# A hybrid Mamba-2 and attention trunk on one core: the decays of the scan leave the high-priority block, and the masked scores get a second buffer

## The chip, the core and the metric

The kernel runs on one core of a Trainium2 chip. The metric is the device time of one execution in microseconds (us); smaller is better. The time before is 2582.29 us, the median of three runs (2581.88 to 2584.90).

## What is computed

A trunk of two layers over 2048 tokens of width 1024, all in float32. The first layer is a Mamba-2 mixer (state-space duality), the second is sliding-window attention. The part that the change touches is the scan of the first layer, chunk by chunk (128 tokens) for each of 8 groups of 4 heads:

```python
a_cs = jnp.cumsum(a, axis=-1)
seg = a_cs[..., :, None] - a_cs[..., None, :]
decay = jnp.exp(jnp.where(causal, seg, -jnp.inf))
cb = jnp.einsum('bclgn,bcsgn->bcgls', Cc, Bc)
y_diag = jnp.einsum('bcgrls,bcsgrp->bclgrp', cb[:, :, :, None] * decay, x)
decay_to_end = jnp.exp(a_cs[..., -1:] - a_cs)
states = jnp.einsum('bclgn,bcgrl,bclgrp->bcgrpn', Bc, decay_to_end, x)
```

The states are carried from chunk to chunk, and `y_off` adds what the carried state gives. Ahead of the scan stand the input projection (1024 to 6176 columns), a causal convolution over 4 tokens and a SiLU; behind it a gate, a norm and the output projection.

## The kernel before, in words

**Stages.** By the trace the first layer's projection and scan take about 0 to 1400 us, its output projection up to about 1725, the attention layer the rest. Every large product is done as three products of split numbers: `mm3` issues high by high (L90), high by low (L92) and low by high (L91) on TensorE (PE). Each weight tile is loaded by SP (L148), rounded to its high part by ScalarE (ACT) as `whi` (L150), and the low part `wlo` is made by GpSimd (POOL, L152).

**Loops.** The first stage runs over two halves of the tokens (hf 0 and 1, 1024 tokens each), and in each over 8 groups. For a group, `ssm_proj` projects the tiles x0, x1, B, C and z0, z1; a tile of x, B or C then goes through the convolution: ACT copies it out of PSUM (L742) and starts the sum (L746), VectorE (DVE) adds the taps (L749), ACT and DVE do the SiLU (L752, L753). The scan of group g runs beside the projection of group g+1: `interleave` steps the generator `ssm_scan` as the projection goes on. The scan of the last group (hf 1, group 7) runs beside the first matmuls of the output projection (`u`, L251), whose weights are split by L222 and L223 and whose rows are squared and summed by a reduction on DVE (L239).

**The scan of one chunk.** `stage1` transposes x0, x1 and B on PE and multiplies B by C into one PSUM tile `pt` (L779 to L784). From it come `xd` (DVE, L789), the split of B into `bh` (ACT, L793) and `bl` (DVE, L795), the weighted inputs `xw` (DVE, L798) and their split `xh` (ACT, L801) and `xl` (DVE, L803), and the masked scores `cbm` (DVE, L806). Then come the decays: four Relu on ACT (L809), the exponential of `ab` (ACT, L814) and its product with C on POOL (L815), the exponential of `dec` (ACT, L816) and its product with `cbm` on DVE (L817). `ab` is a row of cumulated decays that SP's DMA spreads over all partitions (L767). `states` multiplies `xh`, `xl`, `bh`, `bl` on PE into `sps`, two chunks at a time; DVE adds the carried state, `hn` (L842, L844), POOL decays it, `hd` (L833). `outputs` multiplies `dec` by `xd` (L856) and `ab` by the state (L861) into `yt`; DVE and POOL finish it (L868, L870).

**What orders the work.** A scheduler orders each engine's instructions when the program is built. It goes by a priority, which is the place in the program; inside `high_priority(offset=60)` an instruction counts as standing 60 places further ahead. In the kernel before that block reaches from L785 to L817. Each engine then runs its own queue strictly in this order.

**Buffers.** `px` is a ring of four 4 KB buffers for the rows of x (`xt`, L107). `rows` (L574) is loaded once, in the first 20 us, with the convolution's weights and biases and the gate's norm (DMAs L575 to L577); PE transposes it (L579, L582), and DVE scales it to `cw`, `cb` and `gn` (L580, L583, L584). In the kernel before, `rows` has 1 KB per partition of its own, and `cbm` has one buffer of 512 bytes.

Of the kernel before, what the change touches and what calls it, by code (L numbers as in the profile page):

```python
# [11 lines left out]
F32 = mybir.dt.float32  # L12
# [3 lines left out]
AF = mybir.ActivationFunctionType  # L16
ALU = mybir.AluOpType
# [4 lines left out]
P = 128  # L22
T = 2048
D = 1024
# [36 lines left out]
class Trunk:  # L61
# [492 lines left out]
    def ssm_consts(self, pool):  # L554
        nc, io = self.nc, self.io

        def bcast(ap, n, name):
            t = pool.tile([P, n], F32, name=name)
            nc.sync.dma_start(t, ap.partition_broadcast(P))
            return t  # L560

        self.abc = bcast(io["ssm_a_log"][0], NH, "abc")
        nc.scalar.activation(self.abc, self.abc, AF.Exp)
        nc.vector.tensor_scalar(self.abc, self.abc, -1.0, None, ALU.mult)
        self.dtb = bcast(io["ssm_dt_bias"][0], NH, "dtb")
        d = bcast(io["ssm_d"][0], NH, "dall")
        self.dch = pool.tile([P, NH // 2], F32, name="dch")
        d2 = d.rearrange("p (t two) -> p t two", two=2)
        nc.vector.tensor_copy(self.dch[0:64], d2[0:64, :, 0])
        nc.vector.tensor_copy(self.dch[64:P], d2[64:P, :, 1])  # L570

        self.cw = pool.tile([P, 4, 32], F32, name="cw")
        self.cb = pool.tile([P, 32], F32, name="cb")
        rows = pool.tile([P, 2, P], F32, name="rows")  # L574
        nc.sync.dma_start(rows[:, 0, :], io["ssm_conv_w"][0].rearrange("k (t p) -> (k t) p", p=P))  # L575
        nc.sync.dma_start(rows[0:32, 1, :], io["ssm_conv_b"][0].rearrange("(t p) -> t p", p=P))
        nc.sync.dma_start(rows[32:48, 1, :], io["ssm_gate_norm"][0].rearrange("(t p) -> t p", p=P))  # L577
        pt = self.tp.tile([P, P], F32, tag="tr", name="pt")
        nc.tensor.transpose(pt, rows[:, 0, :], self.ident)  # L579
        nc.vector.tensor_scalar(self.cw.rearrange("p k t -> p (k t)"), pt, 0.5, None, ALU.mult)  # L580
        pt = self.tp.tile([P, 48], F32, tag="tr", name="pt")
        nc.tensor.transpose(pt, rows[0:48, 1, :], self.ident[0:48, 0:48])  # L582
        nc.vector.tensor_scalar(self.cb, pt[:, 0:32], 0.5, None, ALU.mult)  # L583
        nc.vector.tensor_scalar(self.gn, pt[:, 32:48], 0.5, None, ALU.mult)  # L584
        self.halo = pool.tile([P, 32, 3], F32, name="halo")
        self.hsave = [pool.tile([P, 256], F32, name=f"hsave{g}") for g in range(NG)]
# [169 lines left out]
    def ssm_scan(self, sp, yp, tabs, hf, g, res, yT):  # L756


        nc = self.nc
        dt, acs, cd, w2, atd = (tabs[k] for k in ("dt", "acs", "cd", "w2", "atd"))  # L760
# [9 lines left out]
        def stage1(c):  # L770
            if c > 7:
                return
            ab = abs_[c]
            s, o = divmod(c, 4)
            sl = slice(o * P, (o + 1) * P)
            x0, x1, Bt, Ct = (res[n, s] for n in ("x0", "x1", "B", "C"))
            pt = (yp.tile([P, 4, P], F32, tag="y", name="pt", bufs=2) if c % 2
                  else self.tp.tile([P, 4, P], F32, tag="tr", name="pt"))
            nc.tensor.transpose(pt[:, 0, :], x0[:, sl], self.ident)  # L779
            nc.tensor.transpose(pt[:, 1, :], x1[:, sl], self.ident)  # L780
            last = hf == 1 and c == 7
            if not last:
                nc.tensor.transpose(pt[:, 2, :], Bt[:, sl], self.ident)
            nc.tensor.matmul(pt[:, 3, :], Bt[:, sl], Ct[:, sl], start=True, stop=True)  # L784
            with self.tc.high_priority(offset=60):  # L785
                xv = pt[:, 0:2, :].rearrange("p a (h d) -> p (a h) d", d=64)
                xd = sp.tile([P, 4, 64], F32, tag="xd", name="xd", bufs=4)
                hb = dt[:, c, 4 * g:4 * g + 4].unsqueeze(2).to_broadcast([P, 4, 64])
                nc.vector.tensor_tensor(xd, xv, hb, ALU.mult)  # L789
                bx = None  # L790
                if not last:
                    bh = sp.tile([P, P], F32R, tag="bh", name="bh")
                    nc.scalar.activation(bh, pt[:, 2, :], AF.Copy)  # L793
                    bl = sp.tile([P, P], F32R, tag="bl", name="bl")
                    nc.vector.tensor_tensor(bl, pt[:, 2, :], bh.bitcast(F32), ALU.subtract)  # L795
                    xw = sp.tile([P, 4, 64], F32, tag="xw", name="xw", bufs=1)
                    hb = w2[:, c, 4 * g:4 * g + 4].unsqueeze(2).to_broadcast([P, 4, 64])
                    nc.vector.tensor_tensor(xw, xv, hb, ALU.mult)  # L798
                    xf = xw.rearrange("p h d -> p (h d)")
                    xh = sp.tile([P, 256], F32R, tag="xh", name="xh")  # L800
                    nc.scalar.activation(xh, xf, AF.Copy)  # L801
                    xl = sp.tile([P, 256], F32R, tag="xl", name="xl")
                    nc.vector.tensor_tensor(xl, xf, xh.bitcast(F32), ALU.subtract)  # L803
                    bx = bh, bl, xh, xl
                cbm = sp.tile([P, P], F32, tag="cbm", name="cbm", bufs=1)
                nc.vector.tensor_tensor(cbm, pt[:, 3, :], self.triu, ALU.mult)  # L806
                dec = sp.tile([P, 4, P], F32, tag="dec", name="dec", bufs=4)
                for r in range(4):
                    nc.scalar.activation(dec[:, r, :], ab[:, r, :], AF.Relu, scale=-1.0,  # L809
                                         bias=acs[:, c, 4 * g + r:4 * g + r + 1])  # L810
                ce = None
                if not (hf == 0 and c == 0):
                    ce = ab
                    nc.scalar.activation(ce, ab, AF.Exp)  # L814
                    nc.gpsimd.tensor_tensor(ce, ce, Ct[:, sl].unsqueeze(1).to_broadcast([P, 4, P]), ALU.mult)  # L815
                nc.scalar.activation(dec, dec, AF.Exp, scale=-1.0)  # L816
                nc.vector.tensor_tensor(dec, dec, cbm.unsqueeze(1).to_broadcast([P, 4, P]), ALU.mult)  # L817
            sts.append((xd, bx, dec, ce))

        def states(c):  # L820
# [54 lines left out]
        for c in range(4):  # L875
            load(c)
        stage1(0)
        yield
        stage1(1)
        yield  # L880
        hprev = self.hsave[g] if hf else None
        hd = decayed(0, hprev)
        yield
        for c in range(0, 8, 2):
            sps = states(c)
            h0 = hprev
            h1, hd = state(c, sps[:, 0, :], hd)
            yield
            hprev, hd = state(c + 1, sps[:, 1, :], hd)
            stage1(c + 2)  # L890
            yield
            stage1(c + 3)
            yield
            outputs(c, (h0, h1))
            load(c + 4)
            load(c + 5)
            yield
# [161 lines left out]
```

## Time and profile before

| | |
|---|---|
| median of 3 runs | 2582.29 us (2581.88 to 2584.90) |
| the profiled execution | 2584.72 us, of which the span of the trace is 2583.0 us |
| PE | 2527.8 us busy, 98% |
| DVE | 1673.7 us busy, 65% |
| ACT | 1274.9 us busy, 49% |
| POOL | 921.6 us busy, 36% |
| DMA | 87 GB/s in the mean |
| TensorE's granted clock | 0.995 of full speed in the mean |

The chain that ended last runs over PE for 74% of the span, over DVE for 10%, POOL 5%, ACT and DMA 4% each. The span is the time between the first and the last instruction in the trace; the rest of the execution's own time lies around it. In the views below an instruction has its start, its duration, its engine, its line, its operation, and what it writes and reads; in square brackets stands how long the engine had been idle before it and whose result ended that.

### The profile page before, as it was taken

The page shows a single profiled execution, that of the slowest core. Times are in us where ns is not written, and L with a number is a line of the kernel's source. Part 1 is how long each engine was busy: PE and PEld are TensorE (multiplying, and loading weights), DVE is VectorE, ACT ScalarE, POOL GpSimd, SP SyncE. Part 2 cuts the span into 40 slices and gives each one's busy share as a digit, 9 for nine tenths or more (in the row PEclk, how much of TensorE's full clock was granted, in tenths as well). Part 3 has the DMA queues.
Part 4 walks back from the last instruction along what each step waited for, and adds up shares of the span by engine and source line. Part 5 has one row for each costly group of instructions (what it writes and reads, how often), then busy time and mean ns, then how long its engine had stood idle before and what let it go on. Part 6 is the DMA issues. An engine that isn't in the chain of part 4 may idle for free.

```text
span 2583.0 us, 38760 instructions
## 1 busy us (share of the span) xinstructions
PE 2527.8 (98%) x14083; PEld 2107.9 (82%) x14083; DVE 1673.7 (65%) x3363; ACT 1274.9 (49%) x3195; POOL 921.6 (36%) x817
## 2 busy tenths in 40 slices
PE   7999999999999999999999999999999999999998
PEld 6878888888777888888887888888888888888787
DVE  6677666766776667666678544447777777767422
ACT  5455555555645555555566422324554455545321
POOL 2344444444434454444445222222222112220222
PEclk9999999999999999999999999999999999999999
DMA  4332223223423222222325332234111121111343
GB/s 127 96 86 64 81 76 87 74 70 78 116 62 105 78 83 77 78 78 78 82 78 174 113 101 90 90 128 140 54 54 58 54 78 54 54 32 58 123 146 120
DMA packets 266656, 224.46 MB, mean 87 GB/s; under 512 B 31136, under 2 KB 229984, under 8 KB 266464
## 3 DMA queue, kind: packets, MB, share of 16 engines
q1 hardware_dynamic: 266464, 221.98, 29.2%
q8 instruction: 111, 1.82, 0.3%
q14 instruction: 81, 0.66, 0.1%
HBM read 179.72 MB, written 42.21 MB: 86 GB/s over the span
## 4 chain that ended last, share of the span: by engine, by line
PE 74%; DVE 10%; POOL 5%; DMA 4%; ACT 4%; issue 4%; SPq 0%; POOLq 0%; ACTq 0%; DVEq 0%
PE u L251 19%; PE ps L90 14%; PE ps L92 14%; PE ps L91 14%; DVE sx L749 2%; DMA ab<-atd 2%; POOL wlo L152 2%; PE sc L420 2%; PE yt L856 2%; PE yt L861 1%; PE ot L474 1%; PE ot L478 1%; DVE dec L817 1%; PE tt L453 1%; POOL ab L815 1%
## 5 line engine op out<-in xcount | busy, mean ns | idle before, releaser
L90 PE MATMUL ps<-hi,whi 128*128 128x512 f32 (+1 forms) x1808 | 725.5, 401 | 9.4 <-ACT whi L150 4.7
L92 PE MATMUL ps<-hi,wlo 128*128 128x512 f32 (+1 forms) x1808 | 706.1, 391 | 4.2 <-POOL wlo L152 4.2
L91 PE MATMUL ps<-lo,whi 128*128 128x512 f32 (+1 forms) x1808 | 704.6, 390 | 0.2 <-DVE lo L140 0.2
L92 PEld LDWEIGHTS ps<-hi,wlo 128*128 128x128 f32 x1808 | 340.7, 188 | 80.2 <-POOL wlo L152 6.1
L90 PEld LDWEIGHTS ps<-hi,whi 128*128 128x128 f32 x1808 | 341.2, 189 | 77.9 <-issue 15.9
L152 POOL TENSOR_TENSOR wlo<-wraw,whi 128x1024 fp32r<-128x1024 f32 x114 | 282.6, 2479 | 319.1 <-ACT whi L150 310.6
L749 DVE SCALAR_TENSOR_TENSOR sx<-raw,cw,sx 128x512 f32<-128x512 f32 x384 | 342.9, 894 | 71.3 <-ACT sx L746 66.5
L91 PEld LDWEIGHTS ps<-lo,whi 128*128 128x128 f32 x1808 | 341.6, 189 | 55.2 <-DVE lo L140 0.8
L251 PE MATMUL u<-ol,yh 128*128 128x512 f32 x768 | 239.6, 393 | 1.0 <-DVE ol L223 0.9
L251 PE MATMUL u<-oh,yh 128*128 128x512 f32 x768 | 240.5, 394 | 0.0
L251 PE MATMUL u<-oh,yl 128*128 128x512 f32 x768 | 237.6, 391 | 0.0
L809 ACT ACTIVATE dec<-ab,acs 128x128 f32<-128x128 f32 x512 | 165.4, 392 | 128.9 <-DMA ab<-atd 114.3
L815 POOL TENSOR_TENSOR ab<-ab,sx 128x512 f32<-128x512 f32 x120 | 168.9, 1409 | 154.5 <-ACT ab L814 140.5
L752 ACT ACTIVATE raw<-sx 128x512 f32<-128x512 f32 x128 | 80.6, 630 | 221.4 <-DVE sx L749 221.3
L90 PE MATMUL ps<-qh,hi 128*128 128x384 f32 x512 | 181.1, 355 | 0.0
L870 POOL TENSOR_TENSOR ysb<-ysb,zz 128x256 f32<-128x256 f32 x128 | 108.1, 861 | 197.9 <-DVE ysb L868 197.7
L235 POOL TENSOR_TENSOR yl<-yr,yh 128x1024 fp32r<-128x1024 f32 (+1 forms) x64 | 119.3, 1864 | 161.3 <-ACT yh L233 161.2
L233 ACT ACTIVATE yh<-yr 128x1024 fp32r<-128x1024 f32 (+1 forms) x64 | 54.1, 845 | 242.3 <-PE u L251 189.3
L91 PE MATMUL ps<-ql,hi 128*128 128x384 f32 x512 | 172.1, 337 | 0.9 <-POOL ql L332 0.9
L251 PEld LDWEIGHTS u<-ol,yh 128*128 128x128 f32 x768 | 143.9, 188 | 34.3 <-DVE ol L223 2.6
L92 PE MATMUL ps<-qh,lo 128*128 128x384 f32 x512 | 171.9, 336 | 0.0
L251 PEld LDWEIGHTS u<-oh,yl 128*128 128x128 f32 x768 | 144.5, 188 | 31.4
(213 smaller groups left out, 4527.7 us busy)
## 6 DMA issues: line engine op xcount, KB each, us to landing
wraw<-in_ssm_w_in SPq DMA_DIRECT2D x98, 512.0 KB, 4.1
ab<-atd SPq DMA_DIRECT2D x128, 256.0 KB, 4.6
xt<-in_x SPq DMA_DIRECT2D x32, 512.0 KB, 4.8
yT<-ysb SPq DMA_DIRECT2D x64, 256.0 KB, 2.5
yr<-yT SPq DMA_DIRECT2D x32, 512.0 KB, 4.0
xt<-x SPq DMA_DIRECT2D x32, 512.0 KB, 4.0
oraw<-in_ssm_w_out SPq DMA_DIRECT2D x16, 512.0 KB, 5.9
x<-xt SPq DMA_DIRECT2D x32, 256.0 KB, 2.1
```

The costliest lines, as they stand in the source:

```text
L90: nc.tensor.matmul(ps, sh, mh, start=first, stop=False)
L91: nc.tensor.matmul(ps, sh, ml, start=False, stop=False)
L92: nc.tensor.matmul(ps, sl, mh, start=False, stop=last)
L152: nc.gpsimd.tensor_tensor(lo, raw, hi.bitcast(F32), ALU.subtract)
L233: nc.scalar.activation(yh, yr, AF.Copy)
L235: nc.gpsimd.tensor_tensor(yl, yr, yh.bitcast(F32), ALU.subtract)
L251: nc.tensor.matmul(st["u"][h], y[:, k, :], w[:, j, 512 * h:512 * h + 512], start=k0 + k == 0 and m == 0, stop=k0 + k == kt - 1 and m == 2)
L749: nc.vector.scalar_tensor_tensor(sx, raw[:, j:j + BLK], self.cw[:, j, ct:ct + 1], sx, ALU.mult, ALU.add)
L752: nc.scalar.activation(th, sx, AF.Tanh)
L809: nc.scalar.activation(dec[:, r, :], ab[:, r, :], AF.Relu, scale=-1.0, bias=acs[:, c, 4 * g + r:4 * g + r + 1])
L815: nc.gpsimd.tensor_tensor(ce, ce, Ct[:, sl].unsqueeze(1).to_broadcast([P, 4, P]), ALU.mult)
L870: nc.gpsimd.tensor_tensor(yv, yv, res[f"z{pr}", s][:, sl], ALU.mult)
```

## The change

Three edits. The high-priority block ends behind `cbm`, so that the decays (the four Relu, both exponentials, POOL's product and DVE's product) are ordered by their own place in the program. `cbm` gets two buffers instead of one. `rows` gives up its own memory and takes a buffer of the ring `px`, which it shares with the rows of x. Nothing is computed differently.

```diff
-        rows = pool.tile([P, 2, P], F32, name="rows")
+        rows = self.px.tile([P, D], F32, tag="px", name="rows")[:, 0:2 * P].rearrange("p (a b) -> p a b", a=2)
...
-                cbm = sp.tile([P, P], F32, tag="cbm", name="cbm", bufs=1)
+                cbm = sp.tile([P, P], F32, tag="cbm", name="cbm", bufs=2)
                 nc.vector.tensor_tensor(cbm, pt[:, 3, :], self.triu, ALU.mult)
-                dec = sp.tile([P, 4, P], F32, tag="dec", name="dec", bufs=4)
-                for r in range(4):
-                    nc.scalar.activation(dec[:, r, :], ab[:, r, :], AF.Relu, scale=-1.0,
-                                         bias=acs[:, c, 4 * g + r:4 * g + r + 1])
-                ce = None
-                if not (hf == 0 and c == 0):
-                    ce = ab
-                    nc.scalar.activation(ce, ab, AF.Exp)
-                    nc.gpsimd.tensor_tensor(ce, ce, Ct[:, sl].unsqueeze(1).to_broadcast([P, 4, P]), ALU.mult)
-                nc.scalar.activation(dec, dec, AF.Exp, scale=-1.0)
-                nc.vector.tensor_tensor(dec, dec, cbm.unsqueeze(1).to_broadcast([P, 4, P]), ALU.mult)
+            dec = sp.tile([P, 4, P], F32, tag="dec", name="dec", bufs=4)
+            for r in range(4):
+                nc.scalar.activation(dec[:, r, :], ab[:, r, :], AF.Relu, scale=-1.0,
+                                     bias=acs[:, c, 4 * g + r:4 * g + r + 1])
+            ce = None
+            if not (hf == 0 and c == 0):
+                ce = ab
+                nc.scalar.activation(ce, ab, AF.Exp)
+                nc.gpsimd.tensor_tensor(ce, ce, Ct[:, sl].unsqueeze(1).to_broadcast([P, 4, P]), ALU.mult)
+            nc.scalar.activation(dec, dec, AF.Exp, scale=-1.0)
+            nc.vector.tensor_tensor(dec, dec, cbm.unsqueeze(1).to_broadcast([P, 4, P]), ALU.mult)
             sts.append((xd, bx, dec, ce))
```

On PE the order stays as it was, but for the first 40 us and for some 40 us around 1390. On the other engines most instructions of the scan move by a place or a few. Three places:

**ACT, where the scan of the first group of the second half starts (about 812 to 819 us).** `whi_8032` is the weight tile that PE needs next, `dec_8005` and `ab_7770` belong to the fourth chunk. First the kernel before, then the changed one:

```order
L814 ACTIVATE ab_7770<-ab_7770 128x512
L801 ACTIVATE xh_7941<-xw_7939 128x256
L816 ACTIVATE dec_8005<-dec_8005 128x512
L752 ACTIVATE raw_7872<-sx_7875 128x512
L744 ACTIVATE halo_345<-ps_7888 128x3
L746 ACTIVATE sx_7960<-ps_7888,cb_333,cw_332 128x512
L150 ACTIVATE whi_8032<-wraw_8030 128x1024
```

```order
L746 ACTIVATE sx_7960<-ps_7888,cb_333,cw_332 128x512
L809 ACTIVATE dec_8005<-ab_7770,acs_7718 128x128 x2
L801 ACTIVATE xh_7941<-xw_7939 128x256
L809 ACTIVATE dec_8005<-ab_7770,acs_7718 128x128
L741 ACTIVATE raw_8020<-halo_345 128x3
L150 ACTIVATE whi_8032<-wraw_8030 128x1024
L814 ACTIVATE ab_7770<-ab_7770 128x512
L816 ACTIVATE dec_8005<-dec_8005 128x512
```

Both exponentials of the fourth chunk stand behind the weight tile now. Further ahead, the SiLU's `raw_7806` (L752) stands ahead of the first chunk's two exponentials instead of behind them, and on DVE the SiLU's L753 stands ahead of the first chunk's L817.

**SP, in the first 30 us.** The three DMAs of `rows` and what stands around them:

```order
 L559 DMA dtb<-in_ssm_dt_bias 128x32
 L559 DMA dall<-in_ssm_d 128x32
+L148 DMA wraw<-in_ssm_w_in 128x8x128 x2
+L107 DMA xt<-in_x 128x1024 x2
 L575 DMA rows<-in_ssm_conv_w 128x128
 L576 DMA rows<-in_ssm_conv_b 32x128
 L577 DMA rows<-in_ssm_gate_norm 16x128
-L148 DMA wraw<-in_ssm_w_in 128x8x128
-L107 DMA xt<-in_x 128x1024
-L148 DMA wraw<-in_ssm_w_in 128x8x128
-L107 DMA xt<-in_x 128x1024
```

They stand behind two weight tiles and two rows of x, and they need a free buffer of `px`: the one whose `xt` PE transposes last before them. On PE, L579 stands four products later, and L582 behind the next transposes of x.

**DVE, beside the output projection (about 1369 to 1373 us).** `red_13343` is the reduction of the output projection, `xl_13420` the split of the sixth chunk of the last group:

```order
 L806 TENSOR_TENSOR cbm_13422<-pt_13405,triu_90 128x128
 L734 SCALAR_TENSOR_TENSOR zz_13433<-zz_13433,ps_13302 128x512
+L239 TENSOR_REDUCE red_13343<-yr_13336 128x128
+L803 TENSOR_TENSOR xl_13420<-xw_13416,xh_13418 128x256
 L817 TENSOR_TENSOR dec_13424<-dec_13424,cbm_13422 128x512
-L803 TENSOR_TENSOR xl_13420<-xw_13416,xh_13418 128x256
-L239 TENSOR_REDUCE red_13343<-yr_13336 128x128
 L844 TENSOR_TENSOR hn_13478<-hd_13453,sps_13471 128x256
```

The reduction has moved ahead of the split, and the product of the decays behind it.

## Rows read from the trace of the kernel before

**Rows 1.** The page's first part: busy us, share of the span, instructions of each engine.
```profile
PE 2527.8 (98%) x14083; PEld 2107.9 (82%) x14083; DVE 1673.7 (65%) x3363; ACT 1274.9 (49%) x3195; POOL 921.6 (36%) x817
```

**Rows 2.** Windows of the second half: length, busy by engine, granted clock, DMA share, GB/s.
```profile
840.00:1340.00 500.00, 499.69 (x2952) 413.00 (x2952) 336.95 (x596) 284.35 (x673) 232.67 (x181) 1.00 0.29 79
```

**Rows 3.** What PE waited for, 100 to 1410 us: sum, times, longest.
```profile
PE sps L91 <- DVE xl L803: 4.8, 9, 1.4
PE ps L90 <- ACT whi L150: 4.7, 2, 2.7
PE ps L92 <- POOL wlo L152: 3.9, 2, 2.2
PE sps L90 <- ACT xh L801: 2.4, 4, 0.8
```

**Rows 4.** Timeline of PE and ACT, first scan of the first half.
```profile
118.95 0.39 PE L91 MATMUL sps<-xl,bh 128*128 128x256 f32 x1 [0.73 <-DVE xl L803]
130.86 0.50 PE L90 MATMUL ps<-hi,whi 128*128 128x512 f32 x1 [2.07 <-ACT whi L150]
...
125.89 0.64 ACT L814 ACTIVATE ab<-ab 128x512 f32<-128x512 f32 x1
126.41 0.64 ACT L816 ACTIVATE dec<-dec 128x512 f32<-128x512 f32 x1
127.89 0.63 ACT L752 ACTIVATE raw<-sx 128x512 f32<-128x512 f32 x1 [0.84 <-DVE sx L749]
129.77 1.04 ACT L150 ACTIVATE whi<-wraw 128x1024 fp32r<-128x1024 f32 x1
```

**Rows 5.** Timeline of DVE, ACT, POOL and PE, first scan of the second half.
```profile
807.71 1.38 DVE L817 TENSOR_TENSOR dec<-dec,cbm 128x512 f32<-128x512 f32 x1 [5.58 <-ACT dec L816]
...
817.86 1.05 ACT L150 ACTIVATE whi<-wraw 128x1024 fp32r<-128x1024 f32 x1
...
818.97 0.50 PE L90 MATMUL ps<-hi,whi 128*128 128x512 f32 x1 [2.66 <-ACT whi L150]
821.45 0.66 PE L92 MATMUL ps<-hi,wlo 128*128 128x512 f32 x1 [1.75 <-POOL wlo L152]
```

**Rows 6.** The window after that wait: columns as in rows 2.
```profile
820.00:825.00 5.00, 3.55 (x20) 2.71 (x22) 5.00 (x8) 2.69 (x6) 2.78 (x2) 0.66 0.40 105
```

**Rows 7.** Timeline of DVE and PE, last pair of chunks, group 7 of the first half.
```profile
768.56 0.68 DVE L817 TENSOR_TENSOR dec<-dec,cbm 128x512 f32<-128x512 f32 x1
...
771.60 0.38 PE L90 MATMUL sps<-xh,bh 128*128 128x256 f32 x1 [0.77 <-ACT xh L801]
772.34 0.39 PE L91 MATMUL sps<-xl,bh 128*128 128x256 f32 x1 [0.36 <-DVE xl L803]
```

**Rows 8.** Timeline of ACT and PE, last pair of chunks, group 0 of the first half.
```profile
175.18 0.28 ACT L793 ACTIVATE bh<-pt 128x128 fp32r<-128x128 f32 x1 [2.08 <-DVE xd L789]
...
176.84 0.38 PE L90 MATMUL sps<-xh,bh 128*128 128x256 f32 x1 [0.82 <-ACT xh L801]
177.58 0.39 PE L91 MATMUL sps<-xl,bh 128*128 128x256 f32 x1 [0.36 <-DVE xl L803]
```

**Rows 9.** Timeline of PE, around the first use of `rows`.
```profile
27.95 0.60 PE L136 MATMUL pt<-ident,xt 128*128 128x128 f32 x4
...
30.73 0.33 PE L579 MATMUL pt<-ident,rows 128*128 128x128 f32 x1 [0.27 <-DVE lo L140]
```

**Rows 10.** DMA issues, 0 to 60 us: count, size, us from issue to landing.
```profile
dtraw<-in_ssm_w_in SPq DMA_DIRECT2D x1, 128.0 KB, 2.8
rows<-in_ssm_conv_w SPq DMA_DIRECT2D x1, 64.0 KB, 4.6
```

**Rows 11.** Timeline of DVE and PE, last scan, beside the output projection.
```profile
1370.77 1.96 DVE L239 TENSOR_REDUCE red<-yr 128x128 f32<-128x1024 f32 x1
...
1370.90 0.39 PE L91 MATMUL sps<-xl,bh 128*128 128x256 f32 x1 [0.76 <-DVE xl L803]
1401.77 0.44 PE L90 MATMUL sps<-xh,bh 128*128 128x256 f32 x1 [2.02 <-DVE hn L844]
```

## The prediction

> **What bounds the kernel now.** I read the page's busy times first, then the stages by windows, then what PE waited for, and last the timelines around the few places where it waited. PE is busy for 2527.8 us, 98% of the span [rows 1]; no other engine passes 65%. So a change that leaves PE's work alone can win no more than PE's idle time, and whatever it does on DVE, ACT and POOL counts only where PE waits for it. By stages the case is clearer still: from 840 to 1340 us, which is most of the second half of the scan, PE is busy for 499.69 of 500 us at the full granted clock [rows 2]. In that stretch the other engines are late for nothing. The waits of the whole stretch that the change touches, 100 to 1410 us, are named in one list [rows 3]: PE waits 4.8 us for `xl`, 4.7 for the high part of a weight tile, 3.9 for its low part, 2.4 for `xh`, and once 2.0 us for the state `hn` [rows 11]. That is 17.8 us in all, 0.7% of the run. The list names neither `dec` nor `cbm` nor the scaled `ab`: PE never waits for the decays. What they can cost is only the place that they take in a queue, ahead of something that PE does wait for. The waits lie at four kinds of places: the start of the scan in either half [rows 4, 5], the last pair of chunks of a group [rows 7, 8], the use of `rows` in the first 40 us [rows 9], and the last scan, beside the output projection [rows 11].
>
> A measurement of this kernel can tell about 0.2%, that is 5.2 us, from no change.
>
> **The change part by part.** Nothing is added to or removed from any engine's work, and no DMA is new. The second `cbm` buffer costs nothing by itself: it lets L806 of a chunk run before L817 of the chunk ahead, which it must, since L817 now stands further back. So everything is order, and I go through the places.
>
> *Start of the scan, first half.* PE stood for 2.07 us until the weight tile `whi` was there, which ACT started at 129.77 [rows 4], and later up to 2.2 us for `wlo` [rows 3], which POOL makes from it. In the new order one L814 and one L816 of the fourth chunk stand behind that tile. They start 0.52 us apart [rows 4], so two of them free 1.04 us. ACT's wait of 0.84 us ahead of L752 [rows 4] shrinks too, since the taps on DVE move ahead of other work; that is between 0 and 0.84. The tile comes 1.04 to 1.88 earlier; I take 1.5. POOL now has one L815 less ahead of `wlo`, so it follows the tile. The `xl` of the second chunk moves ahead of a row of x on DVE, which takes away PE's 0.73 us there [rows 4], but PE then arrives sooner at the same missing tile, so I don't count it. Term: -1.5 us; ends 0 and -4.95 (0.73 + 2.07 + 2.15, all three waits gone).
>
> *Start of the scan, second half.* Here DVE stood 5.58 us before L817 until the first chunk's exponential came, which ACT could not begin before `ab` had landed [rows 5]. Behind that L817 in DVE's queue were `cbm` of the next chunk, the SiLU's L753 and the states. Now L752 and L753 go first. ACT's tile `whi` started at 817.86, and PE waited 2.66 us for it and 1.75 more for `wlo` [rows 5]. Again two exponentials (1.04 us) move behind the tile, and ACT uses a part of the time in which it had stood for `ab` for the L752 that stood behind it (0.5 us, as far apart as the exponentials). That is 1.5 us for `whi`, and `wlo` follows. Term: -1.5; ends 0 and -4.41.
>
> *Last pair of chunks, group 7 of the first half.* PE waited 0.77 for `xh` and 0.36 for `xl` [rows 7]. One L817 of 0.68 us that stood in front of the pair's work [rows 7] now stands behind it. I take the 0.7; ends 0 and -1.13. In the other groups the work on DVE ahead of the last `xl` is the same in sum, only the conv's L753 and the seventh chunk's `xd` change places. There the waits are 0.82 + 0.36 in the first group [rows 8] and smaller ones after it. Term for them: 0; ends -2.3 (what is left of the `xl` and `xh` waits) and, above, the slower rival.
>
> *The first 40 us.* The DMAs of `rows` now wait for a buffer of `px`, which is free when the transposes at 27.95 to 28.55 are done [rows 9]. PE reaches L579 four products later than before. Four transposes take 0.60 us, and before PE waited 0.27 there for something else [rows 9], so that is at 30.73 - 0.27 + 0.60, about 31.0. The bounds of the landing: 4.6 us, as the same DMA took before among large transfers, and 2.8 us, as `dtraw` took when little else ran [rows 10]. So `rows` is there between 31.4 and 33.2, and PE stands 0.4 to 2.2 us. The last row of x is still in flight when it starts, but little comes behind it; I take a value nearer to the lower end: +1.0 us; ends 0 and +2.2. The page "DMA: Bandwidth & Descriptors" of the Trainium skill (section on the anatomy of one DMA, a fit for GpSimd's path) has a fixed 2.0 us and bytes over 436 GB/s; as an estimate from that page, 64 KB would take 2.15 us, land at 30.75, and cost PE nothing, so that the sum below would be 1.0 lower. The trace speaks against it here: no DMA of this size in the first 60 us landed that fast, 2.8 and 4.6 [rows 10], so the rows decide. `rows` holds its slot until L582, and the next load into `px` comes long after, so nothing waits for the slot.
>
> *Beside the output projection.* PE waited 0.76 us for the `xl` that ended at 1370.8 [rows 11]. Now the reduction L239, 1.96 us, stands ahead of this `xl`, and an L817 (0.68, as in [rows 7]) behind it: 1.96 - 0.68 = 1.3 us later, all on PE, which already waits. Term: +1.3; ends 0 and +1.96. The wait of 2.02 at 1401.77 for `hn` [rows 11] hangs on POOL, which gets another order of the same work: 0; ends -2.0 and +1.0 (half of what it is, for want of a nearer row).
>
> *The clock.* From 820 to 825, just behind the wait at the second half's start, the granted clock was 0.66 of full, so about 3.4 of these 5 us were at 1.2 GHz and the rest at 2.4 [rows 6]. Half of the 3.4 us, 1.7, is lost. If a wait becomes short the fall may stay away, at either start; if PE stands longer in the first 40 us one may be added. I count 0; ends -3.4 (both starts) and +1.7.
>
> Sum: -1.5 - 1.5 - 0.7 + 1.0 + 1.3 = -1.4 us. The profiled execution took 2584.72, so 2583.3 on its scale; it stood 2.43 above the median of the runs shown. On the median's scale the forecast is **2580.9 us**, no difference that can be measured.
>
> **The rivals.**
>
> *Faster: the starts come clean.* If the weight tiles come early enough that the clock does not fall at either start (-3.4) and the waits of the last pairs go as well (-2.3), 2580.9 becomes 2575.2, and with a little more of the 4.95 and 4.41 at the starts it is below that. For it: at both starts the waiting chain is ACT's queue alone, and it is ACT's queue that gets shorter. Against: 1.5 us out of 4.2 and 4.4 leaves a wait of over 2.5 us at both, and at the second start the clock fell after a wait of that size [rows 5, 6]. Chance 0.16.
>
> *Slower: the last pairs come late.* In 14 of the 16 groups the seventh chunk's `xd` now stands behind the conv's L753, which itself waits for ACT. `bh` on ACT waited for `xd` in the trace [rows 8], and the last `xl` has no slack there (PE waits for it) [rows 8]. If the whole pair slips by that L753, some 0.68 us (the duration of the L817 in [rows 7], which has as many elements), PE loses 14 times 0.68 = 9.5 us: 2590.4. It decides as soon as `xw` is later than now, for the wait is already there. Against: `bl` and `xw` stood behind the L753 in the old order too, and the second half, 499.69 busy of 500, has room [rows 2]. Chance 0.11.
>
> *Nothing happens.* PE's queue is the same between 40 and 1380 us; if the tiles are bound by DMA or by DVE rather than by ACT's exponentials, the starts stay as they are, and the first 40 us and the reduction cancel against the last pair: 2582.3 to 2584. Chance 0.13; it counts as no change, like the forecast itself with 0.60.
>
> **How the numbers follow.** Faster by over 0.2% is the first rival, 0.16; slower by over 0.2% is the second, 0.11; within it lie the forecast and the empty change, 0.60 + 0.13 = 0.73. The range reaches down to the first rival's 2575 and up to the sum with the clock falling in the first 40 us, a full wait for `rows` and the reduction at its upper end (2580.9 + 1.7 + 1.2 + 0.7 = 2584.5), with another 1.5 for the spread of the runs: 2575 to 2586. It leaves out the slower rival and the far end of the faster one.
>
> **What would show it.** PE's waits for `whi` and `wlo` should fall from 8.6 us to between 5 and 6. The wait for `xl` near 1371 should grow from 0.8 to about 2.1, with L239 right ahead of it. L579 should wait for the DMA of `rows` for about 1 us. From 840 to 1340 PE should stay over 499 us busy. The forecast is wrong if new waits for `dec`, `xd` or `xl` appear in that stretch, if the waits at the starts stay, or if the granted clock falls at a new place.

## The result, and the profile after

The change makes the kernel slower: 2615.55 us, the median of four runs (2614.57 to 2617.50), against 2582.63 us for four runs of the kernel before. The ratio is 1.0127, with a 95% interval of 1.0109 to 1.0144: 33 us. The forecast was 2580.9 us, no difference that can be measured.

The page of the changed kernel, its first part (as in [rows 1]):

```profile
span 2613.4 us, 38766 instructions
PE 2541.3 (97%) x14083; PEld 2115.5 (81%) x14083; DVE 1701.2 (65%) x3363; ACT 1275.3 (49%) x3195; POOL 930.2 (36%) x817
```

The span is 30.4 us longer. PE does the same 14083 matmuls, and its busy time has grown by 13.5 us, which is matmuls at the lower clock or drawn out behind a wait; the rest is new idle time. The mean granted clock fell from 0.995 to 0.992; as an estimate from these two figures, some 26 and 42 us ran at 1.2 GHz and the rest at 2.4, so about 8 of the 13.5 us are the clock's. What PE waited for, 100 to 1410 us (the columns as in [rows 3]):

```profile
PE sps L91 <- DVE xl L803: 10.6, 19, 2.0
PE ps L92 <- POOL wlo L152: 7.8, 4, 2.2
PE sps L90 <- ACT xh L801: 7.6, 9, 1.5
PE ps L90 <- ACT whi L150: 5.9, 3, 3.0
```

The waits for `xl` and `xh` have gone from 7.2 to 18.2 us, from 13 to 28 occurrences; those for the weight tiles, which should have shrunk, from 8.6 to 13.7. And the stretch that was full [rows 2] is so no longer (windows; the third row is a window in the first half, the clock stands behind the five busy times):

```profile
840.00:1340.00 500.00, 492.33 (x2860) 404.25 (x2859) 340.36 (x575) 275.11 (x648) 221.93 (x176) 1.00 0.28 77
150.00:420.00 270.00, 265.67 (x1534) 218.54 (x1533) 186.78 (x339) 150.18 (x353) 119.20 (x90) 0.99 0.28 76
340.00:350.00 10.00, 8.17 (x30) 6.26 (x30) 8.45 (x16) 5.49 (x16) 3.55 (x4) 0.83 0.35 105
```

**Where the time went.** PE transposes B once per chunk (L783), 120 times, in the same sequence in both kernels. The start of the same transpose, before and after, shows how far the changed kernel has fallen behind:

| transpose | before, us | behind by, us | what lies since the row above |
|---|---|---|---|
| 1 | 102.4 | 0.0 | first 40 us, first projection |
| 5 | 146.6 | 0.3 | start of the first half's scan |
| 57 | 696.2 | 13.7 | groups 0 to 6, first half |
| 65 | 790.9 | 11.8 | group 7 |
| 69 | 833.9 | 12.7 | start of the second half's scan |
| 113 | 1333.1 | 25.9 | groups 0 to 6, second half |
| 114 | 1357.8 | 29.3 | start of the last scan |
| 120 | 1389.0 | 29.8 | last scan |

Some 26.6 of 30 us are lost in the steady part, in nearly every group, about 2 us each in the mean. That is the part that the forecast counted at zero.

**How, in the second half.** Take the third pair of chunks of group 3. First PE, DVE and POOL of the kernel before (timeline):

```profile
1077.22 0.39 PE L784 MATMUL pt<-sx 128*128 128x128 f32 x2
...
1077.65 0.42 DVE L789 TENSOR_TENSOR xd<-pt,dt 128x256 f32<-128x256 f32 x1
1082.34 0.75 DVE L749 SCALAR_TENSOR_TENSOR sx<-raw,cw,sx 128x512 f32<-128x512 f32 x1 [4.26 <-ACT sx L746]
1084.39 0.42 DVE L803 TENSOR_TENSOR xl<-xw,xh 128x256 fp32r<-128x256 f32 x1
1085.67 2.55 DVE L749 SCALAR_TENSOR_TENSOR sx<-raw,cw,sx 128x512 f32<-128x512 f32 x1
1089.52 0.42 DVE L803 TENSOR_TENSOR xl<-xw,xh 128x256 fp32r<-128x256 f32 x1
1089.86 0.69 DVE L817 TENSOR_TENSOR dec<-dec,cbm 128x512 f32<-128x512 f32 x1
...
1085.10 2.57 POOL L152 TENSOR_TENSOR wlo<-wraw,whi 128x1024 fp32r<-128x1024 f32 x1 [2.66 <-ACT whi L150]
...
1090.21 0.28 PE L91 MATMUL sps<-xl,bh 128*128 128x256 f32 x1
```

The same place in the changed kernel, with ACT and POOL:

```profile
1094.84 0.39 PE L784 MATMUL pt<-sx 128*128 128x128 f32 x2
...
1094.56 1.28 ACT L809 ACTIVATE dec<-ab,acs 128x128 f32<-128x128 f32 x4 [1.30 <-DMA ab<-atd]
1096.17 0.40 ACT L809 ACTIVATE dec<-ab,acs 128x128 f32<-128x128 f32 x1 [0.33 <-DMA ab<-atd]
1098.05 0.78 ACT L746 ACTIVATE sx<-ps,cb,cw 128x512 f32<-128x512 f32 x1
...
1098.86 3.41 DVE L749 SCALAR_TENSOR_TENSOR sx<-raw,cw,sx 128x512 f32<-128x512 f32 x3 [3.00 <-ACT sx L746]
1102.19 0.41 DVE L789 TENSOR_TENSOR xd<-pt,dt 128x256 f32<-128x256 f32 x1
1105.37 2.30 DVE L803 TENSOR_TENSOR xl<-xw,xh 128x256 fp32r<-128x256 f32 x1
1108.43 0.69 DVE L817 TENSOR_TENSOR dec<-dec,cbm 128x512 f32<-128x512 f32 x1
1109.04 0.42 DVE L803 TENSOR_TENSOR xl<-xw,xh 128x256 fp32r<-128x256 f32 x1
...
1104.93 2.45 POOL L152 TENSOR_TENSOR wlo<-wraw,whi 128x1024 fp32r<-128x1024 f32 x1 [3.20 <-ACT whi L150]
...
1108.70 0.38 PE L90 MATMUL sps<-xh,bh 128*128 128x256 f32 x1 [0.47 <-ACT xh L801]
1109.51 0.38 PE L91 MATMUL sps<-xl,bh 128*128 128x256 f32 x1 [0.43 <-DVE xl L803]
```

Before, DVE makes `xd` as soon as PE has put the chunk into `pt` (1077.65), and the convolution's taps (L749) come behind it. After, the three taps stand ahead of `xd`. DVE stands 3.00 us for ACT's L746; that stands behind Relu that wait for the DMA of `ab`. So `xd` starts at 1102.19, 7 us behind the transposes instead of at once, and what follows it comes late too. In the kernel before the second `xl` was ready at 1089.94 and read at 1090.21: PE did not wait there, but the slack was a quarter of a microsecond. In groups 0 to 5, those in which the three taps moved, the slack at this read was between 0.27 and 2.42 us.

The wait for L746 is not new: in the kernel before DVE stood 4.26 us for it, with `bl`, `xw` and `xl` of the same chunk behind it. What is new ahead of the second `xl` is the second chunk's L817 (1108.43; before it stood behind, at 1089.86), and instructions that last longer beside POOL: the three taps together 3.41 us. The first `xl` falls beside POOL's `wlo` and takes 2.30 us instead of 0.42, but in the kernel before a tap fell there, with 2.55. In groups 0 to 5, from L784 of the pair's first chunk to the end of its second `xl`, the mean grew from 11.19 to 12.66 us by the timelines, while DVE's idle time in it went from 3.12 to 2.55.

**How, in the first half.** Only the last pair of a group makes PE wait there, and it isn't the taps that moved. Take group 3, PE and DVE, the kernel before and then the changed one (timeline):

```profile
408.57 0.39 PE L784 MATMUL pt<-sx 128*128 128x128 f32 x2
...
412.93 1.76 DVE L749 SCALAR_TENSOR_TENSOR sx<-raw,cw,sx 128x512 f32<-128x512 f32 x2
414.61 0.41 DVE L789 TENSOR_TENSOR xd<-pt,dt 128x256 f32<-128x256 f32 x1
415.38 1.01 DVE L753 SCALAR_TENSOR_TENSOR sx<-raw,sx 128x512 f32<-128x512 f32 x1 [0.36 <-ACT raw L752]
...
421.83 0.38 PE L90 MATMUL sps<-xh,bh 128*128 128x256 f32 x1 [0.24 <-ACT xh L801]
```

```profile
414.28 0.39 PE L784 MATMUL pt<-sx 128*128 128x128 f32 x2
...
418.74 0.74 DVE L749 SCALAR_TENSOR_TENSOR sx<-raw,cw,sx 128x512 f32<-128x512 f32 x1
420.32 1.43 DVE L753 SCALAR_TENSOR_TENSOR sx<-raw,sx 128x512 f32<-128x512 f32 x1
421.68 0.41 DVE L789 TENSOR_TENSOR xd<-pt,dt 128x256 f32<-128x256 f32 x1
...
428.53 0.38 PE L90 MATMUL sps<-xh,bh 128*128 128x256 f32 x1 [1.23 <-ACT xh L801]
```

The taps stand ahead of the seventh chunk's `xd` in both kernels. What has moved ahead of it, in groups 0 to 6, is the SiLU's L753, and `xd` starts 7.4 us behind L784 instead of 6.0. There was no slack here: in the kernel before PE read the second `xl` within 0.06 us of its end in every group. From L784 of the pair's first chunk to the end of the second `xl` the mean of groups 0 to 6 grew from 13.25 to 14.59 us with the same instructions; DVE's idle time in it is 1.66 and 1.67 us, so the whole growth is instructions that last longer. PE waits up to 1.47 us for `xh` and 0.36 for `xl` at the last pair, and near 344 us, behind the longest of these waits, the clock falls as well (the window above with 0.83).

### The profile page after: what moved, and what is told of

Same layout as the page of the kernel before. It is cut to its first block, busy times and chain, and to the rows that moved or that the text cites. A ratio compares the mean times of both kernels' runs of the same rounds, so it can differ in the third digit from the quotient of the medians.

```text
span 2613.4 us, 38766 instructions
## 1 busy us (share of the span) xinstructions
PE 2541.3 (97%) x14083; PEld 2115.5 (81%) x14083; DVE 1701.2 (65%) x3363; ACT 1275.3 (49%) x3195; POOL 930.2 (36%) x817
## 4 chain that ended last, share of the span: by engine, by line
PE 66%; DVE 11%; POOL 7%; issue 6%; ACT 5%; DMA 4%; SPq 0%; POOLq 0%; ACTq 0%; DVEq 0%
PE u L251 19%; PE ps L90 12%; PE ps L92 12%; PE ps L91 12%; DMA ab<-atd 3%; POOL wlo L152 3%; DVE sx L749 2%; POOL ab L815 2%; PE sc L420 2%; DVE xl L803 2%; PE ot L474 1%; PE yt L856 1%; POOL hd L833 1%; DVE dec L817 1%; PE ot L478 1%
## 5 line engine op out<-in xcount | busy, mean ns | idle before, releaser
L749 DVE SCALAR_TENSOR_TENSOR sx<-raw,cw,sx 128x512 f32<-128x512 f32 x384 | 345.9, 902 | 100.2 <-ACT sx L746 95.7
L152 POOL TENSOR_TENSOR wlo<-wraw,whi 128x1024 fp32r<-128x1024 f32 x114 | 288.5, 2530 | 324.2 <-ACT whi L150 323.6
L752 ACT ACTIVATE raw<-sx 128x512 f32<-128x512 f32 x128 | 80.8, 631 | 232.8 <-DVE sx L749 232.8
```

Of the source, the lines that this page charges most:

```text
L152: nc.gpsimd.tensor_tensor(lo, raw, hi.bitcast(F32), ALU.subtract)
L749: nc.vector.scalar_tensor_tensor(sx, raw[:, j:j + BLK], self.cw[:, j, ct:ct + 1], sx, ALU.mult, ALU.add)
L752: nc.scalar.activation(th, sx, AF.Tanh)
```

## Experiments

Theory A: the order on DVE, the convolution's taps ahead of `xd`, is the loss; the decays cause it only by leaving ACT's queue, so that the convolution passes them there. Theory B: the memory (`rows` in `px`, second `cbm` buffer). Theory C: the late decays or DVE's product themselves. Each ratio is against the kernel before on the same chip, with its 95% interval. Lines of e4 and e7 to e10 stand one to thirteen further down than in the kernel before (taps L751, `xd` L798, `xl` L812).

**e1: only `rows` moved.**

```diff
-        rows = pool.tile([P, 2, P], F32, name="rows")
+        rows = self.px.tile([P, D], F32, tag="px", name="rows")[:, 0:2 * P].rearrange("p (a b) -> p a b", a=2)
```

> The kernel before, with only `rows` moved into the ring px (cbm one buffer, decays in the block). Theory A (the order on DVE: the convolution's taps, which wait for ACT, now stand ahead of the states and of xd): this edit has no part in it, 2583 us within 3. Theory B (the memory: `rows` in px holds up the first loads, and the second cbm buffer reorders DVE): some of the 33 us show here, 2588 us or more. In the first 40 us both expect PE to end within 1 us of before.

Measured: 2582.20 us, ratio 1.0008 (0.9999 to 1.0017). The first transpose of a chunk starts 0.3 us later than before. `rows` has no part in the loss that these runs can tell.

**e2: only the decays leave the block.**

```diff
-                cbm = sp.tile([P, P], F32, tag="cbm", name="cbm", bufs=2)
+                cbm = sp.tile([P, P], F32, tag="cbm", name="cbm", bufs=1)
...
-        rows = self.px.tile([P, D], F32, tag="px", name="rows")[:, 0:2 * P].rearrange("p (a b) -> p a b", a=2)
+        rows = pool.tile([P, 2, P], F32, name="rows")
```

(against the changed kernel)

> The kernel before, with only the decays taken out of the high-priority block (cbm one buffer, `rows` in its own memory). Theory A: all of the loss is here, 2615 us within 4, with PE's waits for xl and xh at 15 us or more between 100 and 1410 us (7.2 before). Theory B: the loss needs the second cbm buffer, 2583 to 2595 us.

Measured: 2608.53 us, ratio 1.0106 (1.0092 to 1.0120). PE's waits of this kernel, 100 to 1410 us:

```profile
PE sps L91 <- DVE xl L803: 10.7, 22, 1.8
PE sps L90 <- ACT xh L801: 8.1, 9, 1.5
```

18.8 us of waits, as A had it, but the time is 2.5 us below A's range: most of the loss, not all, is here (see e12).

**e3: only DVE's product leaves the block.**

```diff
                 nc.scalar.activation(dec, dec, AF.Exp, scale=-1.0)
-                nc.vector.tensor_tensor(dec, dec, cbm.unsqueeze(1).to_broadcast([P, 4, P]), ALU.mult)
+            nc.vector.tensor_tensor(dec, dec, cbm.unsqueeze(1).to_broadcast([P, 4, P]), ALU.mult)
```

(against the kernel before; `rows` and `cbm` as in the changed one)

> The changed kernel, but only DVE's product of the decays (L817) leaves the high-priority block; the Relu, both exponentials and POOL's product stay in it. Theory A says that the loss comes from ACT: its convolution instructions pass the decays there, and so the taps pass xd on DVE. So this kernel stays near the kernel before, 2583 us within 5. Theory C (DVE's product, late or stretched beside POOL, is what delays xl): the loss is kept, 2605 us or more.

Measured: 2586.92 us, ratio 1.0017 (1.0008 to 1.0026). PE is busy for all of 840 to 1340 us. The product's place alone costs some 4 us against the kernel before, clear of the noise, but not the 33. The rest hangs on the leaving of the Relu, the exponentials and POOL's product.

**e4: the taps put behind `xd`.** The convolution hands its taps and SiLU over instead of issuing them, and the scan issues them once the next `xd` is in the program, on DVE behind it.

```diff
+            def finish(raw=raw, sx=sx, ct=ct):
...
+            if self.pend:
+                self.pend()
+            self.pend = finish
...
-                nc.vector.tensor_tensor(xd, xv, hb, ALU.mult)
+                xi = nc.vector.tensor_tensor(xd, xv, hb, ALU.mult)
...
+            if self.pend:
+                with self.tc.issue_after(xi.ins):
+                    self.pend()
+                self.pend = None
             sts.append((xd, bx, dec, ce))
```

> The changed kernel, decays out of the block, but the convolution's taps and SiLU of a tile (L749 to L753) are put into the program behind the next chunk's xd, and DVE issues them behind it. Theory A: with xd ahead of the taps again the waits for xl and xh between 840 and 1340 us go back to under 1 us (7 in the changed kernel), and the time to 2583 to 2593 us. Theory C, or any theory by which the late decays themselves are the loss: the time stays at 2610 us or more.

Measured: 2578.58 us, ratio 0.9994 (0.9986 to 1.0003). All of the 33 us are back, and more than A expected (2583 at the least). The windows of this kernel:

```profile
840.00:1340.00 500.00, 500.00 (x2949) 413.71 (x2948) 342.78 (x593) 286.51 (x671) 226.79 (x181) 1.00 0.28 78
```

The decays are out of the block as in the changed kernel, and PE is full: that they leave is not by itself the loss. But they aren't as late in time here. The product L817 ends 6.4 us behind its chunk's L784 in the mean of all chunks, against 7.5 in the changed kernel and 7.0 before. And e4 does more than undo the move: it puts taps and SiLU further back than they stood in the kernel before. So against theory C stands e4 together with two other things: PE's list of waits in the changed kernel has none for `dec`, and e5 has the loss with the decays in their block.

**e5: the kernel before, with `xd` forced behind the taps.**

```diff
-                nc.vector.scalar_tensor_tensor(sx, raw[:, j:j + BLK], self.cw[:, j, ct:ct + 1],
+                self.tap = nc.vector.scalar_tensor_tensor(sx, raw[:, j:j + BLK], self.cw[:, j, ct:ct + 1],
...
-                nc.vector.tensor_tensor(xd, xv, hb, ALU.mult)
+                    with self.tc.issue_after(self.tap.ins):
+                        nc.vector.tensor_tensor(xd, xv, hb, ALU.mult)
```

> The kernel before in everything, decays in the block, but DVE must issue each chunk's xd behind the convolution's taps that the program has ahead of it. Theory A (it is this order on DVE that costs, not the decays): slower by 15 us or more, 2597 us at least, with PE waiting for xl and xh in many groups. If the decays' own lateness were needed for the loss, this stays at 2582 us within 5.

Measured: 2629.69 us, ratio 1.0186 (1.0167 to 1.0206). PE's waits, 100 to 1410 us (L808 and L806 are `xl` and `xh` here):

```profile
PE sps L92 <- DVE xl L808: 19.6, 24, 2.1
PE sps L91 <- ACT xh L806: 14.3, 12, 2.9
```

With the decays in their block, this order alone costs 47 us. It is more than the change costs; here the second and the eighth chunk's `xd` stand behind two or three more taps too. Theory A stands from both sides: taking the order away brings the time back, putting it in alone brings a loss.

**e6: the Relu back in the block, the rest out.**

```diff
+            with self.tc.high_priority(offset=60):
+                dec = sp.tile([P, 4, P], F32, tag="dec", name="dec", bufs=4)
+                for r in range(4):
+                    nc.scalar.activation(dec[:, r, :], ab[:, r, :], AF.Relu, scale=-1.0,
...
```

(against the changed kernel)

> The changed kernel with the four Relu back in the high-priority block; both exponentials and both products stay out. The exponentials are what the convolution's L742 and L746 pass on ACT, and in the order that results the taps stand ahead of xd just as in the changed kernel. So Theory A expects most of the loss: 2600 to 2616 us. If the Relu were what matters, 2583 to 2588 us.

Measured: 2613.29 us, ratio 1.0126 (1.0111 to 1.0141), as A had it. But it falls behind at other places: 1.9 us at transpose 56, 3.0 at 69 and 20.2 at 113. So in the second half the exponentials' leaving is enough; in the first half the Relu have to leave too. DVE's order in the trace fits that: in the first half L753 is back behind the seventh chunk's `xd` in every group, and in the second half the three taps still stand ahead of the fifth chunk's in groups 1 to 5 (two of them in group 0). So by the order in the trace L753 makes the first half's loss and the taps make the second's. In the first half one tap more than before stands ahead of the fifth chunk's `xd`, here as in the changed kernel; the 1.9 us are all that it can have cost.

**e7 and e8: what the decays' place is worth once the taps are behind `xd`.** e7 is the kernel before with the edit of e4; e8 is e2 with it (decays out, one `cbm` buffer, own `rows`).

> The kernel before (decays in the block, one cbm buffer, own rows) with the taps behind xd as in e4. If the taps' place is all that matters, the same as e4, 2578 to 2581 us. If e4 won something because its decays are out of the block, this one is 2 us or more above e4.

> As e4 (decays out, taps behind xd) with one cbm buffer and rows in its own memory. If the second buffer is of use once the taps are in their place, this is slower than e4 by 2 us or more; if not, 2577 to 2581 us.

Measured: e7 2581.88 us, ratio 1.0001 (0.9992 to 1.0010); e8 2577.86 us, ratio 0.9987 (0.9978 to 0.9996). So e7 is 3.3 us above e4 and 4.0 above e8, and e8 is level with e4: the decays' leaving seems to win a few us once nothing is lost by it (the intervals of e7 and e8 still touch, from 0.9992 to 0.9996), and the second buffer isn't needed for that. PE at the starts of the two scans in e8 (timeline; `whi` is L151, `wlo` L153):

```profile
127.63 0.50 PE L91 MATMUL ps<-hi,whi 128*128 128x512 f32 x1 [0.19 <-ACT whi L151]
130.21 0.50 PE L93 MATMUL ps<-hi,wlo 128*128 128x512 f32 x1 [1.85 <-POOL wlo L153]
...
809.17 0.50 PE L91 MATMUL ps<-hi,whi 128*128 128x512 f32 x1 [0.31 <-ACT whi L151]
811.87 0.50 PE L93 MATMUL ps<-hi,wlo 128*128 128x512 f32 x1 [1.96 <-POOL wlo L153]
```

The waits for `whi`, 2.07 and 2.66 us before [rows 4, 5], are 0.19 and 0.31. In e7 they are 2.3 us together:

```profile
PE ps L91 <- ACT whi L151: 2.3, 2, 1.4
```

So about half of this gain comes with the taps' place, and 1.8 us with the decays' leaving, which the forecast had priced; the waits for `wlo` are 3.9 us in e7 and 3.8 in e8.

**e9 and e10: going on from e8.** e9 puts the taps behind `xw` instead of `xd`; e10 keeps e8 and puts the product of the decays behind `xl`:

```diff
+            with self.tc.issue_after(xli.ins):
-            nc.vector.tensor_tensor(dec, dec, cbm.unsqueeze(1).to_broadcast([P, 4, P]), ALU.mult)
+                nc.vector.tensor_tensor(dec, dec, cbm.unsqueeze(1).to_broadcast([P, 4, P]), ALU.mult)
```

> As e8, but the taps are put behind xw (L798 of the old numbering) instead of xd, so that bl and xw cannot be held up by them either. In e8 PE still waits 5.3 us for xl and xh, 3.7 of it in the last scan. If the taps are part of that, 2575 us or less; if what is left hangs on other work (the output projection's DVE work, the weight tiles), the same as e8 within 2 us.

> As e8, and DVE issues the product of the decays (L817) of a chunk behind the chunk's xl. PE waits for xl and never for the product while PE is full, so no wait should be added, and the waits for xl in the last scan (1.6 and 0.4 us) may go: 2575 to 2578 us. If the product, now later, makes PE wait at yt, 2580 us or more.

Measured: e9 2583.19 us, ratio 1.0004 (0.9995 to 1.0013), 5 us above e8, which neither branch had; why was not followed up. e10 2576.47 us, ratio 0.9981 (0.9973 to 0.9990). That is the fastest version of this study, faster than both kernels; against e8 (0.9978 to 0.9996) the intervals overlap.

**e11 and e12: the rest of the loss.** The changed kernel again, and with one `cbm` buffer.

> The changed kernel again, on the same chip as e12: 2615 us within 4.

> The changed kernel with one cbm buffer again (rows stay in px). e2 (one buffer, own rows) took 2608.5 us, 7 less than the changed kernel. If the second buffer makes that difference, this takes 2608 us within 3; if `rows` in px does, 2615 us within 3.

Measured: e11 2612.76 us, ratio 1.0120 (1.0102 to 1.0138); e12 2609.52 us, ratio 1.0109 (1.0093 to 1.0125). The second buffer may cost some 3 us on top; the intervals overlap, so this stays open.

## Why the prediction was wrong

**What bounds the kernel: right, and read too far.** PE is the bound, and only its waits count. But from 499.69 busy of 500 us [rows 2] the forecast concluded that the other engines are "late for nothing" and that the second half "has room". A full PE says that nothing is late; it does not say by how much. The slack is the distance between the end of a write and the matmul that reads it. For the second `xl` of the pair above it was 0.27 us in the kernel before (1089.94 to 1090.21), and no view of waits shows that. The forecast's own sign of being wrong came: between 840 and 1340 us PE waits 6.4 us for `xl` and 1.0 for `xh`.

**The step that failed** is the sentence on the other groups, "the work on DVE ahead of the last `xl` is the same in sum, only the conv's L753 and the seventh chunk's `xd` change places", priced at 0. The second part holds for the first half alone. In groups 0 to 5 of the second half three taps moved ahead of the fifth chunk's `xd`, one tap and an L753 ahead of the sixth's, and one L817 ahead of the second `xl`. The first part counted instructions and not their time: in the first half's last pairs the same instructions came out 1.3 us later, with no more idle time on DVE, since more of them fell beside POOL's work. The runs put about 26.6 us in this place; some 1.8 of them are one wait for a weight tile's `wlo` near 677 us. e5 shows that such an order makes a loss, e4 that without it all of the loss is gone, and e6 parts the two halves.

**The slower rival** had the place and, for the first half, the very step: `xd` behind L753, and no slack at the last `xl`, at a chance of 0.11. By the trace it is 13 groups, not 14. Its size was too small, 9.5 us, one L753 of 0.68 in each group: in group 3 `xd` came 1.4 us later, the first half's seven groups alone lost 13.4 us, and the clock fell behind the waits. The taps of the second half it did not have. Its argument against, the room in the second half, was the mistake above.

**The starts of the scans: the right mechanism, measured only without the loss.** In the changed kernel ACT started the first tile at 129.80, as before at 129.77 [rows 4]:

```profile
126.85 0.63 ACT L752 ACTIVATE raw<-sx 128x512 f32<-128x512 f32 x1 [1.33 <-DVE sx L749]
129.80 1.04 ACT L150 ACTIVATE whi<-wraw 128x1024 fp32r<-128x1024 f32 x1
```

Two exponentials are behind it, but L752 stood 1.33 us for taps instead of 0.84, which the forecast had shrinking, and ACT was already 0.57 us later at the L742 near 112 us (112.04 instead of 111.47). PE, earlier by the `xl` wait that did go, waited 3.02 us instead of 2.07. At the second half's start the waits went from 4.41 to 3.91 us, where -1.5 was forecast. In e8 the transposes around either start gain 3.6 and 3.7 us; in e7, where the decays stay in the block, 2.1 and 1.1. The difference, 1.6 and 2.6 us, is the decays' leaving and near the 1.5 each of the forecast.

**The last pair of group 7:** forecast -0.7; the two waits [rows 7] are gone, and the table shows 1.9 us made up over that group.

**The first 40 us:** forecast +1.0, measured 0.0. The DMA issues of the changed kernel (the last number is the median us to landing):

```profile
rows<-in_ssm_conv_w SPq DMA_DIRECT2D x1, 64.0 KB, 2.1
rows<-in_ssm_conv_b SPq DMA_DIRECT2D x1, 16.0 KB, 2.5
```

and its PE where `rows` is read (timeline):

```profile
30.87 0.33 PE L579 MATMUL pt<-ident,rows 128*128 128x128 f32 x1
33.14 0.26 PE L582 MATMUL pt<-ident,rows 48*128 48x48 f32 x1 [0.80 <-DVE cw L580]
```

`rows` was issued at 28.51, about when forecast, and landed in 2.1 us, below both rows that bounded it (2.8 and 4.6 [rows 10]). Here the estimate from the Trainium skill, "DMA: Bandwidth & Descriptors" (the anatomy of one DMA), 2.15 us, was the better one, and the sentence that the trace speaks against it was wrong: the rows it rested on were transfers among others or larger ones. It held for this one DMA; the 16 KB one, 2.04 by the same estimate, took 2.5.

**Beside the output projection:** forecast a wait of about 2.1 us for that `xl`; measured 1.99:

```profile
1399.40 0.58 PE L91 MATMUL sps<-xl,bh 128*128 128x256 f32 x1 [1.99 <-DVE xl L803]
```

L239 stands right ahead of it, as forecast, so this term was right. Of the waits near it, the 1.40 us for the `xl` ahead of it are gone, and `yt` waits 1.36 us for `cbm` at 1425. What was missed is the last weight tile ahead of it: PE waits 1.14 us for `whi` and 1.70 for `wlo` near 1375, since on ACT that tile now stands behind an L752 that waited 2.57 us for taps. Together they are 2.8 of the 3.4 us between transposes 113 and 114.

## What to carry to other kernels

An engine that is 100% busy tells nothing of the slack behind it: before work is moved in a queue that feeds it, take the distance between each late producer's end and its reader's start, here 0.27 us at one place and 0.06 at another. When instructions change places in an in-order queue, the same count of work is not the same time: ask of each instruction that moved ahead whom it waits for, and beside what it will then run. And a lower priority of one kind of work is a higher one of another: what moved ahead, the convolution, was never named in the edit, and fixing its place behind one instruction (e4) turned the same edit from 1.3% slower into no slower, and with own buffers into 0.13% faster (e8).

## What the runs showed of the hardware

DVE's `xl`, which reads two tiles in SBUF, lasts about as long as POOL's `wlo` where it falls beside it: it took 2.30 us at 1105.37, ending at 1107.67, and `wlo`, begun at 1104.93, ended at 1107.38. In the changed kernel's scan each of the 86 `xl` with no POOL instruction beside them took 0.41 to 0.43 us; 34 fell beside one, with a median of 2.59. The taps took 0.73 to 0.75 us with none beside them (209 of them), and up to 2.51 beside one. `xw`, which reads PSUM, took 0.41 us beside POOL as alone. So an instruction that slides by a microsecond can grow by two. The small DMAs of `rows` landed in 1.7 to 2.5 us with little other traffic, and in 4.1 to 4.6 us among large transfers in the kernel before.
